# A two-layer trunk on one core: row normalisations and combined blocks at the ends of stages

## The chip, the cores and the metric

The kernel runs on one core of a Trainium2 chip. The engines of the core are TensorE (PE, matmuls), VectorE (DVE), ScalarE (ACT), GpSimd (POOL) and SyncE (SP, which issues most DMAs). Each engine works through its own queue strictly in order, and waits on semaphores for results of the others. The metric is the device time of one execution in microseconds (us), and lower is better.

## The reference

The input is one sequence of 1024 tokens, 1024 wide, in fp32, and a conditioning vector. Two layers follow each other. Each has a mixer (layer 0 a gated delta net, layer 1 a retention) and a feed-forward network, with adaptive gains; after each of the two a row normalisation is done. Cut to what the change touches:

```
DN_ALPHA = (2.0 * DEPTH) ** 0.25

def _standardize(x, eps):
    mu = jnp.mean(x, axis=-1, keepdims=True)
    xc = x - mu
    return xc * lax.rsqrt(jnp.mean(xc * xc, axis=-1, keepdims=True) + eps)

# a sublayer: residual, gained output, row normalisation
x = standardize(DN_ALPHA * x + gain * sublayer(modulated(x)))
# the feed-forward network
g, u = split(h @ ffn_up);  y = (silu(causal_dwconv(g)) * u) @ ffn_down
# after the last sublayer
out = standardize(...) * g + b
```

## The kernel before

Operands of matmuls are split into a high and a low part (`split`, L89 makes the high one by ACT, L90 the low one by DVE, or by POOL where asked), and each product is three matmuls, high by low, low by high and high by high (L110 to L112, L315 to L317, L616). Rows are tiled by 128: 8 row tiles, in two halves of four. Columns are cut in two halves of 512. PSUM tiles have the names `acc`, `sc` (accumulators) and `mm` (two banks, for transposes and short products). A scheduler has laid down the order of every engine's queue by its own estimate of when things are ready; on the chip the order is fixed.

The stages that matter, with their place in the profiled execution:

- **Delta net out projection** (`proj_ln`, L301 to L355, about 660 to 761 us). It runs for half 0 and half 1, in each for two column halves `nh`; four accumulators `accs[t]`, one for each row tile. When an accumulator is done, L345 multiplies it by the gain into `t`, and `add_row` (L283, DVE) makes ALPHA times the residual row plus `t` and, in the same instruction, the row's sum. `row_stats` (L286 to L292): DVE turns the sums into a negative mean, ACT squares both halves with an accumulated sum (L289), DVE brings that to a variance, POOL raises it to the power of minus one half (L292). `normalize` then runs on ACT (L297, 128x1024, bias from L296) or on DVE (L299). The residual rows come by DMA (`load_row`, L273) into buffers of the name `lane`. While half 1 is projected, `hooks` for half 0 are put between its groups of matmuls: transposes of the finished rows (L259, PE, into `mm`), scale and shift (L261, ACT), split into `hT` (L89, L90).
- **Start of a feed-forward network** (`strassen`, about 761 to 837 us in layer 0, 2305 to 2377 us in layer 1). The up projection is done with products of blocks, after Winograd. For the first two items both left halves are computed plainly from `hT`, while `build_T` (L373 to L418) transposes the rows of the second half (L387), scales them (L389, ACT: blocks `12` and `22`) and makes four combined blocks T1 to T4 of each `k` (L409 to L415). A sum of high and low part of a block that exists only split is made on PE by two matmuls with a unit matrix (`joined`, L395). All four combined blocks of `k` are made before those of `k + 1`. From the third item on each goes through `wino`: seven products with the blocks, of which the first two need `11` and `21`, the third T1, the fourth T2, the sixth T3, the seventh T4. Each needs a combined weight block, which DVE makes (`psub`, L1184, in an `mm` bank) and splits (L90, `wb`). Beside that, DVE works off the short convolution of the gate (L1527), the join of its halves (L1513) and adaptive gains of the next stage (`ada`, L214 and L216). The first sum in `wino` is taken when both the product in `sc` is done (L1513) and a copy by ACT.
- **End** (second part of `proj_gen`, about 2957 to 2990 us). The seventh product of the last down projection gives four accumulators one after the other, for row tiles 0 to 3 of the second half and the low column half. For each, `f4` adds it to a partial result (L1397), multiplies by the gain (L1398), `add_row` adds the residual, `norm` does `row_stats`, and the two column halves go apart: the low one by two DVE operations (L1355, L1356), the high one by ACT (L1354) and two POOL operations with gain and bias rows (L1358, L1359). Two DMAs per row tile bring them out (L1357, L1360).

Of the kernel before, what the change touches and what calls it, by code (L numbers as in the profile page):

```python
# [33 lines left out]
def trunk_kernel(ctx: ExitStack, tc, A):  # L34
# [250 lines left out]
    def row_stats(st, xt):  # L285
# [6 lines left out]
        pool.tensor_tensor(st[:, 3:4], st[:, 4:5], mhalf[:, 0:1], ALU.pow)  # L292

    def normalize(xt, st, on_act):
        if on_act:
            dve.tensor_tensor(st[:, 2:3], st[:, 2:3], st[:, 3:4], ALU.mult)  # L296
            act.activation(xt, xt, AF.Identity, bias=st[:, 2:3], scale=st[:, 3:4])  # L297
        else:
            dve.tensor_scalar(xt, xt, st[:, 2:3], st[:, 3:4], ALU.add, ALU.mult)  # L299

    def proj_ln(half, nk, get_hl, wsrc, xsrc, G, key=None, final=None, hooks=(), per=2, tag="lane", done=None):  # L301
# [5 lines left out]
        else:  # L307
            hooks = [h for p in zip(loads, hooks[:4]) for h in p] + hooks[4:] if hooks else loads
        stats = [flat(tl("st", [P, 2, 6])) for _ in range(4)]

# [8 lines left out]
        for nh in range(2):  # L319
# [21 lines left out]
            for t in range(4):  # L341
                for n, (hl, w, kk) in enumerate(tail):
                    mmt(accs[t], t, hl, w, kk, False, n == 3)
                tmp = tl("t2", [P, HALF])
                dve.tensor_mul(tmp, accs[t], G[nh])  # L345
# [26 lines left out]

    def build_T(B, xts, scale, shift, tags):  # L373
        tags = dict(zip(("T1", "T2", "T3", "T4", "22"), tags))
# [24 lines left out]
        for k, tg in enumerate((("qkv", "qkv"), ("qkv", "qkv"), ("t2", "t2"), ("t2", "ada"))):  # L399
            b12, b22 = load(k, tg[0]), load(4 + k, tg[1])  # L400
            put("12", k, b12, pool if BAL["b3"] & 1 << k else dve)
            put("22", k, b22, pool if BAL["b2"] & 1 << k else dve)
            raw.append((b12, b22))

        def rest():
            for k in range(4):
                t1, b22 = raw[k]
                x11 = joined(B["11"][k])
# [722 lines left out]

    def strassen(hT0, xts, scale, shift, items, tags=("hTb", "hTb", "qkv", "qkv", "aux"), direct=False, beside=None):
        B = {"11": hT0[:4], "21": hT0[4:]}
# [18 lines left out]
        for n in range(2):  # L1152
# [7 lines left out]
            for t, x in zip(ahead[n], X):  # L1160
                act.activation(t, x, AF.Copy)
        rest = build_T(B, xts, scale, shift, tags)

# [55 lines left out]

        bg_tag[0] = "lane"  # L1220
        for n in range(2):
# [25 lines left out]
    def proj_gen(nj, ablk, wsrc, slots, xsrc, G, final, ln_next, tag, ltags, dst, key, mm=pe.matmul, gate=None, gain=None):  # L1247
# [87 lines left out]
        def xload(half, t):  # L1335
# [32 lines left out]
        def gained(half, t, nh, c):  # L1368
            later.append(lambda: dve.tensor_tensor(c, c, G[nh], ALU.mult))
            later.append(lambda: finish(half, t, nh, c))  # L1370

        def f1(t, acc):
# [22 lines left out]

        def f4(t, acc):
            dve.tensor_tensor(p1[t], acc, p1[t], ALU.add)  # L1397
            dve.tensor_tensor(p1[t], p1[t], G[0], ALU.mult)  # L1398
            finish(1, t, 0, p1[t])
            norm(1, t)  # L1400
# [77 lines left out]
    def layer_tail(i, mix, wout, xsrc, x_mid, x_out, ln_next, final):  # L1478
        sc2, sh2 = fold(i, 1, 2 * i)
        if i == 0:  # L1480
            hT0 = []
            get = out_hl(mix)
            G1 = rows[0, 2]
            xts = proj_ln(0, GH, get, wout, xsrc, G1, ("x", i))
            hooks = ln_hooks(0, xts, "hTa", lambda: (sc2, sh2), hT0, x_mid, ("mid", i), BAL["gh"])
            xts = proj_ln(1, GH, get, wout, xsrc, G1, ("x", i), hooks=hooks)
            hooks = ln_hooks(1, xts, "hTa", lambda: (sc2, sh2), [], x_mid, ("mid", i))
            for h in hooks[KT:]:
                h()
        else:  # L1490
            mix.append((sc2, sh2))
            hT0, xts = proj_st(mix[0])
# [6 lines left out]
        ad = dr.tile([NF // 2, 7, P, HALF], F32, tag=f"ad{i}", name=f"ad{i}")  # L1499
        up = A["ffn_up"][i]  # L1500

        def pair_items(fp):
            g, o = [], []

            def gate_start():
                g.extend(tl("lane", [P, D], name="g") for _ in range(2))

# [426 lines left out]
```

## Time and profile before

| what | value |
| --- | --- |
| median of 3 runs | 2995.94 us (2995.53 to 2998.75) |
| the profiled execution | 2992.3 us |
| its span, first to last instruction | 2990.3 us |
| PE busy, share of the span | 95% |
| DVE busy | 73% |
| ACT busy | 45% |
| POOL busy | 20% |
| mean granted TensorE clock | 0.980 |

Rows of groups and of the timeline read: start, duration, engine, line, operation, output from input, shape, count, and in brackets how long the engine stood idle just before and what released it. Rows of waits read: engine, output and line, what it waited for, then us in total, times, and the longest. `L12` is line 12 of the kernel; the lines of the changed kernel are some 5 to 52 higher.

### The profile page before, as it was taken

What the parts mean: (1) busy time and instruction counts of PE and PEld (TensorE: products, weight loads), DVE (VectorE), ACT (ScalarE), POOL (GpSimd) and SP (SyncE); (2) the same over time, 40 slices, a digit from 0 to 9 for tenths busy, and PEclk for the clock granted to TensorE, in tenths of its full rate; (3) what the DMA queues carried; (4) which work ended last, traced back from release to release, by engine and by line L of the source; (5) the groups of instructions that cost most, each with busy time, mean ns of one, the idle gap of its engine ahead of it and who ended that gap; (6) DMA issues with size and microseconds to landing.
All of it is one profiled execution on the core that took longest, in us unless ns stands there. A gap on an engine that the chain in (4) does not pass through costs nothing.

```text
span 2990.3 us, 38893 instructions
## 1 busy us (share of the span) xinstructions
PE 2827.8 (95%) x13638; PEld 2308.4 (77%) x13638; DVE 2191.9 (73%) x3877; ACT 1347.4 (45%) x2513; POOL 604.6 (20%) x629
## 2 busy tenths in 40 slices
PE   8889998999999999999999989989999899999996
PEld 7768877887778888877787777767778688888785
DVE  5785687545588888997677665656687787778888
ACT  4655555434544444536443333212345544445444
POOL 0411221133011111520002330232201011112603
PEclk9999999999999999999999999999999999999998
DMA  7222221344344444864424453556573333335652
GB/s 273 86 77 72 96 89 64 117 159 137 110 141 162 155 151 147 311 204 135 154 79 145 157 210 119 170 169 183 169 248 125 127 134 106 106 106 200 242 179 106
DMA packets 235379, 442.35 MB, mean 148 GB/s; under 512 B 22192, under 2 KB 75696, under 8 KB 235184
## 3 DMA queue, kind: packets, MB, share of 16 engines
q1 hardware_dynamic: 205024, 387.96, 38.9%
q10 hardware_dynamic: 25152, 34.61, 3.2%
q0 software_dynamic: 5008, 17.30, 1.5%
q8 instruction: 107, 1.75, 0.2%
q14 instruction: 88, 0.72, 0.1%
HBM read 331.26 MB, written 108.53 MB: 147 GB/s over the span
## 4 chain that ended last, share of the span: by engine, by line
PE 68%; DVE 13%; issue 8%; DMA 6%; ACT 4%; POOL 2%; SPq 0%; POOLq 0%; ACTq 0%; DVEq 0%
PE acc L616 15%; PE acc L1412 11%; PE acc L1138 8%; PE acc L110 5%; PE acc L111 4%; PE acc L112 4%; PE sc L616 4%; PE sc L1138 3%; PE sc L1412 3%; PE mm L616 2%; PE sc L111 2%; PE sc L110 2%; PE sc L112 2%; DMA mvw<-in_ada_w 1%; DVE qkv L435 1%
## 5 line engine op out<-in xcount | busy, mean ns | idle before, releaser
L1412 PE MATMUL acc<-bb,ab 128*128 128x512 f32 x1800 | 427.7, 392 | 3.7 <-DVE bb L90 1.5
L1412 PEld LDWEIGHTS acc<-bb,ab 128*128 128x128 f32 x1800 | 337.3, 188 | 78.2 <-DVE bb L90 3.9
L616 PE MATMUL acc<-hT,wh 128*128 128x512 f32 x960 | 301.2, 395 | 0.0
L1548 POOL TENSOR_TENSOR o<-o 128x512 f32<-128x512 f32 x88 | 118.3, 1354 | 719.5 <-DVE o L1541 684.7
L1138 PE MATMUL acc<-T,wb 128*128 128x512 f32 x840 | 209.4, 400 | 12.6 <-DVE wb L90 12.6
L616 PEld LDWEIGHTS acc<-hT,wh 128*128 128x128 f32 x960 | 183.4, 191 | 33.8
L616 PE MATMUL acc<-hT,wl 128*128 128x512 f32 x480 | 203.5, 424 | 0.2 <-ACT sg L1064 0.2
L89 ACT ACTIVATE ab<-ar 128x512 fp32r<-128x512 f32 x210 | 129.4, 624 | 158.7 <-PE acc L1412 85.6
L1138 PEld LDWEIGHTS acc<-T,wb 128*128 128x128 f32 x840 | 161.2, 193 | 50.6 <-DVE wb L90 16.9
L90 DVE TENSOR_TENSOR ab<-ar,ab 128x512 fp32r<-128x512 f32 x210 | 172.9, 830 | 30.1 <-ACT ab L89 29.7
L90 DVE TENSOR_TENSOR wb<-wr,wb 128x512 fp32r<-128x512 f32 x162 | 114.2, 710 | 86.8 <-ACT wb L89 86.5
L90 DVE TENSOR_TENSOR wl<-wr,wh 128x1024 fp32r<-128x1024 f32 x85 | 104.2, 1225 | 97.3 <-ACT wh L89 97.3
L89 ACT ACTIVATE wh<-wr 128x1024 fp32r<-128x1024 f32 x101 | 106.8, 1058 | 129.9 <-PE acc L616 61.5
L90 DVE TENSOR_TENSOR wb<-mm,wb 128x512 fp32r<-128x512 f32 x216 | 145.1, 685 | 21.1 <-ACT wb L89 19.1
L1197 ACT ACTIVATE pc<-acc 128x512 f32<-128x512 f32 x143 | 84.6, 592 | 160.9 <-PE acc L1138 108.2
L89 ACT ACTIVATE wb<-mm 128x512 fp32r<-128x512 f32 x216 | 122.4, 593 | 76.5 <-DVE mm L1184 76.2
L89 ACT ACTIVATE wb<-wr 128x512 fp32r<-128x512 f32 x162 | 98.9, 626 | 98.8 <-DMA wr<-in_ffn_up 49.5
L616 PE MATMUL acc<-wh,hT 128*128 128x512 f32 x384 | 137.1, 420 | 2.5 <-DVE vv L90 1.6
L1527 DVE SCALAR_TENSOR_TENSOR o<-g,vc,o 128x512 f32<-128x512 f32 (+2 forms) x176 | 135.3, 787 | 0.9 <-ACT o L1522 0.2
L435 DVE SCALAR_TENSOR_TENSOR qkv<-raw,vc,qkv 128x512 f32<-128x512 f32 x144 | 114.8, 801 | 26.8 <-ACT qkv L433 25.5
L216 DVE SCALAR_TENSOR_TENSOR ada<-mvw,e,ada 128x512 f32<-128x512 f32 x140 | 107.1, 765 | 27.2 <-DMA mvw<-in_ada_w 27.1
L110 PE MATMUL acc<-T,wb 128*128 128x512 f32 x292 | 116.7, 400 | 9.9 <-DVE wb L90 9.4
(620 smaller groups left out, 7079.8 us busy)
## 6 DMA issues: line engine op xcount, KB each, us to landing
wr<-in_ffn_up SPq DMA_DIRECT2D x96, 512.0 KB, 4.4
mvw<-in_ada_w SPq DMA_DIRECT2D x80, 512.0 KB, 4.4
ad<-o SPq DMA_DIRECT2D x154, 256.0 KB, 2.3
ar<-ad SPq DMA_DIRECT2D x154, 256.0 KB, 4.0
Br<-in_ffn_down SPq DMA_DIRECT2D x66, 256.0 KB, 3.8
wr<-in_ret_wv SPq DMA_DIRECT2D x32, 512.0 KB, 3.9
ar<-od SPq DMA_DIRECT2D x56, 256.0 KB, 5.2
xs<-xt ACTq DMA_DIRECT2D x24, 512.0 KB, 3.1
```

What stands on the lines that cost most here:

```text
L89: act.activation(dst_h, src, AF.Copy)
L90: eng.tensor_tensor(dst_l, src, dst_h, ALU.subtract)
L110: mm(acc, wl[:, k], hl[0], start=first, stop=False)
L111: mm(acc, wh[:, k], hl[1], start=False, stop=False)
L112: mm(acc, wh[:, k], hl[0], start=False, stop=last)
L216: dve.scalar_tensor_tensor(a, wr[:, kk], e[:, k:k + 1], a, ALU.mult, ALU.add)
L435: dve.scalar_tensor_tensor(oh, raw[:, 3 - j:515 - j], w[:, 3 - j:4 - j], oh, ALU.mult, ALU.add)
L616: pq(pe.matmul(out, lhsT, rhs, start=start, stop=stop, **kw), cost)
L1138: return pe.matmul(*a, skip_group_check=True, **kw)
L1412: mm_ = (lambda *a, p=p, onto=onto, **kw: (mm if p < 2 else pe.matmul)(*a, skip_group_check=onto, **kw))
L1527: dve.scalar_tensor_tensor(tv, gv[:, c0 - j:c1 - j], w[:, 2 - j:3 - j], tv, ALU.mult, ALU.add)
L1548: pool.tensor_tensor(o[d], o[x], o[y], op)
```

## The change

Four things are changed. What is computed stays the same, apart from the order of sums.

1. In the out projection of layer 0 (`proj_ln`), a row's sum and squares are no longer made by L283, L289 and ACT. DVE adds the residual without a sum (L352 of the changed kernel), takes `bn_stats` of each column half (L353), joins them with `bn_aggr`, adds epsilon; POOL makes the power; and DVE normalises the 128x1024 row (L357), where ACT did (L297).
2. At the end, row tiles 2 and 3 of the second half use DVE alone but for POOL's power: `bn_stats`, and the gain and bias for both column halves in two operations each (L1373, L1375). Their partial result is multiplied by the gain and added to the residual ahead of the last product (`before_last`), so that after it stand L1444 (accumulator times gain), L1445 (add), L1368 (`bn_stats`).
3. The rows of half 1 in `proj_ln` lie in buffers of the name `aux` instead of `lane`, with their loads spread among the first hooks; in layer 0 the block `22` goes to `lane`, and the gate's tiles and the background tiles to `aux`.
4. `build_T` makes the combined blocks by the order of use in both feed-forward networks: T1 for all four `k`, then T2, T3, T4. T3 joins block `11` a second time, so that 24 unit-matrix matmuls stand in the start of each network instead of 16. The retention keeps the old order.

```
+    def row_bn(st, xt, mv):
+        dve.bn_aggr(mv[:, 0:2], st)
+        dve.tensor_scalar(mv[:, 2:3], mv[:, 1:2], LN_EPS, None, ALU.add)
+        pool.tensor_tensor(mv[:, 3:4], mv[:, 2:3], mhalf[:, 0:1], ALU.pow)
...
-                add_row(stats[t], nh, xv, tmp)
+                dve.scalar_tensor_tensor(xv, xv, ALPHA, tmp, ALU.mult, ALU.add)
+                dve.bn_stats(stats[t][:, nh], xv)
                 if nh == 1:
-                    row_stats(stats[t], xts[t])
-                    normalize(xts[t], stats[t], BAL["gn"] & 1 << half)
+                    mv = tl("s8", [P, 4], name="mv")
+                    row_bn(stats[t], xts[t], mv)
+                    dve.tensor_scalar(xts[t], xts[t], mv[:, 0:1], mv[:, 3:4], ALU.subtract, ALU.mult)
...
+            for k, (t1, b22) in enumerate(raw):
+                dve.tensor_sub(t1, t1, joined(B["11"][k]))
+                put("T1", k, t1)
+            for k, (t1, b22) in enumerate(raw):
                 dve.tensor_sub(b22, b22, t1)
-                put("T3", k, b22, pool if BAL["b3"] & 1 << k else dve)
-                dve.tensor_add(b22, b22, x11)
-                put("T2", k, b22, pool if BAL["bT"] & 1 << k else dve)
-                dve.tensor_sub(t1, t1, x11)
-                put("T1", k, t1, pool if BAL["b1"] & 1 << k else dve)
+                put("T2", k, b22)
+            for k, (t1, b22) in enumerate(raw):
+                dve.tensor_sub(t1, b22, joined(B["11"][k]))
+                put("T3", k, t1)
+            for k, (t1, b22) in enumerate(raw):
                 dve.tensor_sub(b22, joined(B["21"][k]), b22)
-                put("T4", k, b22, pool if BAL["b4"] & 1 << k else dve)
+                put("T4", k, b22)
...
+        def last_rows(t):
+            xt, st = xts[1][t], stats[1][t]
+            mv = tl("s8", [P, 4], name="mv")
+            dve.bn_stats(st[:, 0:6], xt[:, hs(0)])
+            row_bn(st.rearrange("p (a b) -> p a b", a=2), xt, mv)
+            (gB, bB), out = final
+            r0 = HALF + t * P
+            for h2 in range(2):
+                dve.scalar_tensor_tensor(xt[:, hs(h2)], xt[:, hs(h2)], mv[:, 0:1], gB[h2], ALU.subtract, ALU.mult)
+            for h2 in range(2):
+                dve.scalar_tensor_tensor(xt[:, hs(h2)], xt[:, hs(h2)], mv[:, 3:4], bB[h2], ALU.mult, ALU.add)
+                sp.dma_start(out[r0:r0 + P, hs(h2)], xt[:, hs(h2)])
+
+        def late(half, t):
+            return final and half and t > 1
+
+        def before_last(t):
+            lo, hi = xts[1][t][:, hs(0)], xts[1][t][:, hs(1)]
+            dve.bn_stats(stats[1][t][:, 6:12], hi)
+            dve.tensor_tensor(p1[t], p1[t], G[0], ALU.mult)
+            dve.scalar_tensor_tensor(lo, lo, ALPHA, p1[t], ALU.mult, ALU.add)
...
         def f4(t, acc):
+            if late(1, t):
+                lo = xts[1][t][:, hs(0)]
+                dve.tensor_tensor(p1[t], acc, G[0], ALU.mult)
+                dve.tensor_tensor(lo, lo, p1[t], ALU.add)
+                last_rows(t)
+                return
             dve.tensor_tensor(p1[t], acc, p1[t], ALU.add)
...
-            xts = proj_ln(1, GH, get, wout, xsrc, G1, ("x", i), hooks=hooks)
+            xts = proj_ln(1, GH, get, wout, xsrc, G1, ("x", i), hooks=hooks, tag="aux")
...
+        spare = ("aux", "lane")[i]
...
-        strassen(hT0, xts, sc2, sh2, [it for fp in range(NF // 2) for it in pair_items(fp)])
+        strassen(hT0, xts, sc2, sh2, [it for fp in range(NF // 2) for it in pair_items(fp)], ("hTb", "hTb", "qkv", "qkv", ("lane", "aux")[i]), spare=spare)
```

How the order of the queues changes is shown at three places.

**VectorE in the out projection**, where half 1's first column half ends. `hT` rows split transposed rows of half 0; L345 (L350 after the change) frees an accumulator. Before:

```order
L90 TENSOR_TENSOR hT<-t_6605,hT 128x512
L90 TENSOR_TENSOR hT<-t_6615,hT 128x512
L90 TENSOR_TENSOR hT<-t_6637,hT 128x512
L345 TENSOR_TENSOR t_6676<-acc,g_6025 128x512
L345 TENSOR_TENSOR t_6691<-acc,g_6025 128x512
L90 TENSOR_TENSOR hT<-t_6647,hT 128x512
L283 SCALAR_TENSOR_TENSOR xt,st<-xt,t_6676 128x512
```

and with the change:

```order
L357 TENSOR_SCALAR xt<-xt,mv 128x1024 x3
L90 TENSOR_TENSOR hT<-t_6503,hT 128x512
L90 TENSOR_TENSOR hT<-t_6551,hT 128x512
L350 TENSOR_TENSOR t_6616<-acc,g_6025 128x512
L352 SCALAR_TENSOR_TENSOR xt<-xt,t_6616 128x512
L353 BN_STATS st<-xt 128x6
L90 TENSOR_TENSOR hT<-t_6575,hT 128x512
L350 TENSOR_TENSOR t_6632<-acc,g_6025 128x512
L350 TENSOR_TENSOR t_6648<-acc,g_6025 128x512
L90 TENSOR_TENSOR hT<-t_6599,hT 128x512
```

Seven splits of `hT` stood ahead of the first L345, and two stand ahead of it now; the normalisation of three rows of half 0 (L357) has come in ahead of them.

**The start of the feed-forward network of layer 1**, TensorE first. `sc` is the product of blocks `21` that runs when the plain products are through, `mm` what a join leaves, and `acc<-T1` the first product with a combined block. Before, from the last join on (ten more rows of the product in `sc` follow):

```order
L395 MATMUL mm_20234<-hT_19537,ident_r_727 128x512 x2
L112 MATMUL acc_20348<-hT_19464,wb_20345 128x512
L110 MATMUL acc_20348<-hT_19474,wb_20345 128x512
L111 MATMUL acc_20348<-hT_19474,wb_20345 128x512
L112 MATMUL acc_20348<-hT_19474,wb_20345 128x512
L111 MATMUL sc_20368<-hT_19507,wb_20365 128x512
```

and with the change:

```order
L402 MATMUL mm_20218<-hT_19507,ident_r_727 128x512 x2
L110 MATMUL sc_20360<-hT_19507,wb_20357 128x512
L402 MATMUL mm_20226<-hT_19517,ident_r_727 128x512 x2
L111 MATMUL sc_20360<-hT_19507,wb_20357 128x512
L112 MATMUL sc_20360<-hT_19507,wb_20357 128x512
L110 MATMUL sc_20360<-hT_19517,wb_20357 128x512
L111 MATMUL sc_20360<-hT_19517,wb_20357 128x512
L112 MATMUL sc_20360<-hT_19517,wb_20357 128x512
L110 MATMUL acc_20379<-T1_20130,wb_20376 128x512
```

Behind the last join stood 15 matmuls up to the end of the product in `sc`; now there are five.

VectorE at the same place, up to the split of the weight block that the first product with T1 needs (`wb`, last row). Before:

```order
L415 TENSOR_TENSOR bt_20070<-mm_20234,bt_20070 128x512
L1184 TENSOR_TENSOR mm_20382<-mm_20363,wr_20341 128x512
L90 TENSOR_TENSOR T4_20239<-bt_20070,T4_20238 128x512
L1527 SCALAR_TENSOR_TENSOR o_20242<-g_20078,vc_153,o_20242 128x511
L1513 TENSOR_TENSOR g_20339<-sc_20368,pc_20361 128x512
L1527 SCALAR_TENSOR_TENSOR o_20247<-g_20078,vc_153,o_20247 128x512
L1527 SCALAR_TENSOR_TENSOR o_20242<-g_20078,vc_153,o_20242 128x510
L1527 SCALAR_TENSOR_TENSOR o_20252<-g_20079,vc_153,o_20252 128x511
L1527 SCALAR_TENSOR_TENSOR o_20257<-g_20079,vc_153,o_20257 128x512
L1527 SCALAR_TENSOR_TENSOR o_20247<-g_20078,vc_153,o_20247 128x512
L90 TENSOR_TENSOR wb_20384<-mm_20363,wb_20384 128x512
```

and with the change (ahead of these rows stand the two L436, of which the second takes `mm_20226`, one L1205 and a split of T4):

```order
L1565 TENSOR_TENSOR g_20331<-sc_20360,pc_20353 128x512
L1205 TENSOR_TENSOR mm_20374<-mm_20355,wr_20333 128x512
L90 TENSOR_TENSOR T4_20231<-bt_20050,T4_20230 128x512
L1579 SCALAR_TENSOR_TENSOR o_20234<-g_20058,vc_153,o_20234 128x511
L1579 SCALAR_TENSOR_TENSOR o_20239<-g_20058,vc_153,o_20239 128x512
L1579 SCALAR_TENSOR_TENSOR o_20244<-g_20059,vc_153,o_20244 128x511
L214 TENSOR_SCALAR ada_20431<-mvw_20432,e_162 128x512
L1579 SCALAR_TENSOR_TENSOR o_20249<-g_20059,vc_153,o_20249 128x512
L1579 SCALAR_TENSOR_TENSOR o_20234<-g_20058,vc_153,o_20234 128x510
L1579 SCALAR_TENSOR_TENSOR o_20475<-g_20331,vc_153,o_20475 128x511
L1579 SCALAR_TENSOR_TENSOR o_20239<-g_20058,vc_153,o_20239 128x512
L90 TENSOR_TENSOR wb_20376<-mm_20355,wb_20376 128x512
```

Between the row that reads `sc` (L1513, now L1565) and `wb` stood five rows, and now there are ten. In layer 0 both engines' rows stand in the same order.

**VectorE at the end of the program**, from the read of the last accumulator on. Before (the row that reads it is L1397):

```order
L1397 TENSOR_TENSOR pa<-acc,pa 128x512
L1355 SCALAR_TENSOR_TENSOR xt<-xt,st,rowb 128x512
L1398 TENSOR_TENSOR pa<-pa,rowb 128x512
L290 TENSOR_TENSOR st<-st 128x1
L283 SCALAR_TENSOR_TENSOR xt,st<-xt,pa 128x512
L291 TENSOR_SCALAR st<-st 128x1
L286 TENSOR_TENSOR st<-st 128x1
L287 TENSOR_SCALAR st<-st 128x1
L1355 SCALAR_TENSOR_TENSOR xt<-xt,st,rowb 128x512
L1353 TENSOR_TENSOR st<-st 128x1
```

and with the change, to the program's last row (the row that reads it is L1444):

```order
L1444 TENSOR_TENSOR pa<-acc,rowb 128x512
L296 TENSOR_SCALAR mv<-mv 128x1
L1373 SCALAR_TENSOR_TENSOR xt<-xt,mv,rowb 128x512 x2
L1445 TENSOR_TENSOR xt<-xt,pa 128x512
L1375 SCALAR_TENSOR_TENSOR xt<-xt,mv,rowb 128x512 x2
L1368 BN_STATS st<-xt 128x6
L295 BN_AGGR mv<-st 128x2
L296 TENSOR_SCALAR mv<-mv 128x1
L1373 SCALAR_TENSOR_TENSOR xt<-xt,mv,rowb 128x512 x2
L1375 SCALAR_TENSOR_TENSOR xt<-xt,mv,rowb 128x512 x2
```

Eleven operations of 128x512 elements lead VectorE from the last accumulator to the program's last row: seven for tile 3, and four (the first L1373 and L1375 pairs) that still belong to tile 2. Before, ACT and POOL did the high half of each of these rows.

More of the change, by code (lines that the diff above doesn't have):

```diff
@@ L308, in proj_ln @@
             hooks = [h for p in zip(loads, hooks[:4]) for h in p] + hooks[4:] if hooks else loads
-        stats = [flat(tl("st", [P, 2, 6])) for _ in range(4)]
+        stats = [tl("st", [P, 2, 6]) for _ in range(4)]
         def mmt(acc, t, hl, w, kk, first, last):
@@ L400, in build_T @@
             b12, b22 = load(k, tg[0]), load(4 + k, tg[1])
-            put("12", k, b12, pool if BAL["b3"] & 1 << k else dve)
-            put("22", k, b22, pool if BAL["b2"] & 1 << k else dve)
+            put("12", k, b12)
+            put("22", k, b22)
             raw.append((b12, b22))
         def rest():
-            for k in range(4):
-                t1, b22 = raw[k]
-                x11 = joined(B["11"][k])
-                dve.tensor_sub(b22, b22, t1)
-                put("T3", k, b22, pool if BAL["b3"] & 1 << k else dve)
-                dve.tensor_add(b22, b22, x11)
-                put("T2", k, b22, pool if BAL["bT"] & 1 << k else dve)
-                dve.tensor_sub(t1, t1, x11)
-                put("T1", k, t1, pool if BAL["b1"] & 1 << k else dve)
+            if direct:
+                for k in range(4):
+                    t1, b22 = raw[k]
+                    x11 = joined(B["11"][k])
+                    dve.tensor_sub(b22, b22, t1)
+                    put("T3", k, b22)
+                    dve.tensor_add(b22, b22, x11)
+                    put("T2", k, b22)
+                    dve.tensor_sub(t1, t1, x11)
+                    put("T1", k, t1)
+                    dve.tensor_sub(b22, joined(B["21"][k]), b22)
+                    put("T4", k, b22)
+                return
+            for k, (t1, b22) in enumerate(raw):
+                dve.tensor_sub(t1, t1, joined(B["11"][k]))
+                put("T1", k, t1)
+            for k, (t1, b22) in enumerate(raw):
+                dve.tensor_sub(b22, b22, t1)
+                put("T2", k, b22)
+            for k, (t1, b22) in enumerate(raw):
+                dve.tensor_sub(t1, b22, joined(B["11"][k]))
+                put("T3", k, t1)
+            for k, (t1, b22) in enumerate(raw):
                 dve.tensor_sub(b22, joined(B["21"][k]), b22)
-                put("T4", k, b22, pool if BAL["b4"] & 1 << k else dve)
+                put("T4", k, b22)
         return rest
@@ L1130, in c_of, with strassen @@
         return b
-    def strassen(hT0, xts, scale, shift, items, tags=("hTb", "hTb", "qkv", "qkv", "aux"), direct=False, beside=None):
+    def strassen(hT0, xts, scale, shift, items, tags=("hTb", "hTb", "qkv", "qkv", "aux"), direct=False, beside=None, spare="lane"):
         B = {"11": hT0[:4], "21": hT0[4:]}
@@ L1218, in wino @@
             bg_step()
-        bg_tag[0] = "lane"
+        bg_tag[0] = spare
         for n in range(2):
@@ L1370, in gained @@
             later.append(lambda: finish(half, t, nh, c))
+            if late(half, t):
+                later.append(lambda: before_last(t))
         def f1(t, acc):
@@ L1505, in gate_start @@
             def gate_start():
-                g.extend(tl("lane", [P, D], name="g") for _ in range(2))
+                g.extend(tl(spare, [P, D], name="g") for _ in range(2))
                 def gate(q, a, b):
```

5 lines of the change are left out of this document (3 added, 2 removed).

## The prediction

> **What bounds the kernel now.** I read the page's shares first, then TensorE's waits, then the timelines of PE and DVE at the stages that the change touches.
>
> ```profile
> PE 2827.8 (95%) x13638; PEld 2308.4 (77%) x13638; DVE 2191.9 (73%) x3877; ACT 1347.4 (45%) x2513; POOL 604.6 (20%) x629
> ```
>
> TensorE is busy for 95% of the span, so a change that leaves its matmuls alone can only take out its gaps. The waits of PE from 700 to 870 us (us in total, times, longest) cover the out projection and the start of the first feed-forward network:
>
> ```profile
> PE acc L110 <- DVE wb L90: 4.7, 1, 4.7
> PE acc L315 <- DVE t L345: 3.2, 2, 2.5
> PE mm L259 <- ACT t L261: 2.6, 3, 1.1
> PE mm L387 <- ACT bt L389: 2.1, 1, 2.1
> PE acc L1138 <- DVE wb L90: 1.9, 1, 1.9
> ```
>
> The first and last row belong to the combined blocks; the second and third are the out projection, the fourth the first transposes of the network. PE's timeline shows what the longest wait in the out projection brings with it:
>
> ```profile
> 735.73 0.80 PE L315 MATMUL acc<-wh,hl 128*128 128x512 f32 x1 [2.46 <-DVE t L345]
> 736.32 0.63 PE L316 MATMUL acc<-wl,hl 128*128 128x512 f32 x1
> 736.75 0.63 PE L317 MATMUL acc<-wh,hl 128*128 128x512 f32 x1
> ...
> 741.87 0.44 PE L317 MATMUL acc<-wh,hl 128*128 128x512 f32 x1
> 742.14 0.39 PE L315 MATMUL acc<-wh,hl 128*128 128x512 f32 x1
> 742.37 0.39 PE L316 MATMUL acc<-wl,hl 128*128 128x512 f32 x1
> ```
>
> After 2.46 us of waiting the matmuls follow each other at 0.43 us until 741.87, and then at 0.23: some 15 matmuls lose 0.2 us each, 3.0 us on top of the wait. [...]
>
> **The change part by part.**
>
> *(a) Out projection.* DVE's rows ahead of that matmul:
>
> ```profile
> 733.78 1.29 DVE L90 TENSOR_TENSOR hT<-t,hT 128x512 fp32r<-128x512 f32 x2 [1.08 <-ACT hT L89]
> 734.99 1.28 DVE L345 TENSOR_TENSOR t<-acc,g 128x512 f32<-128x512 f32 x2
> ```
>
> L345, which frees the accumulator, stood behind seven splits of `hT`, each waiting for ACT. With the change two are ahead of it, so it can run some five splits (5 x 0.64 = 3.2 us) sooner, which is more than the wait of 2.46. If so, wait and slow matmuls go: 2.46 + 3.0 = 5.5. Of the 2.6 us of L259's waits on ACT I take a fifth, 0.5, since the transposes now stand in smaller groups. What DVE gets for it, per row tile two `bn_stats` and a normalisation, costs by their nearest rows:
>
> ```profile
> L1761 DVE BATCH_NORM_STATS2 rst<-sc x32: 685/699/700, 1836.2 to 2161.4; 128x6 f32<-128x512 f32 x32
> L299 DVE TENSOR_SCALAR xt<-xt,st x12: 806/812/816, 1447.0 to 2318.2; 128x1024 f32<-128x1024 f32 x12
> 727.00:761.00 34.00, 28.84 (x122) 22.74 (x121) 13.01 (x25) 11.47 (x16) 7.15 (x3) 0.90 0.40 137
> ```
>
> That is 2 x 0.70 + 0.81 = 2.2 us a tile, 18 us for eight tiles over two halves; in the window row (DVE's busy time is the third, 13.01 of 34 us) they fit in idle time. Three normalisations (2.4 us) are now ahead of L350, however: if they come late, since each waits for POOL's power, the wait stays. So -6, from -9 (3.2 + 2.6 + 3.0, all of it) to -2 (only the lesser waits go).
>
> DVE and POOL do hold each other up:
>
> ```profile
> 702.44 2.39 POOL L90 TENSOR_TENSOR wl<-wr,wh 128x1024 fp32r<-128x1024 f32 x1 [3.04 <-ACT wh L89]
> 702.47 2.92 DVE L283 SCALAR_TENSOR_TENSOR xt<-xt,t 128x512 f32<-128x512 f32 x1
> ```
>
> An L283 that starts with POOL's split ends with it, 2.92 us where other operations of its size take 0.69 (L1513, below). L352, in its place, has the same two operands in SBUF, and keeps that price; `bn_stats` and L357 have one. [...]
>
> *(b) Buffers at the first network's start.*
>
> ```profile
> 785.83 1.79 PE L387 MATMUL mm<-cst,xt 128*128 128x128 f32 x8 [2.08 <-ACT bt L389]
> ```
>
> ```profile
> PE mm L387 <- ACT bt L389: 0.7, 1, 0.7
> ```
>
> The first row is from PE's timeline, the last from PE's waits from 2300 to 2400 us, the same place in layer 1. In layer 0 ACT's first two block builds stood behind both last copies of the plain products (L1161); with the rows in other buffers they come ahead of the last copy, as they already did in layer 1, where PE waits 0.7. The wait of 2.08 and some half-clock matmuls behind it go: -2.5, from -3.5 to 0.
>
> *(c) Combined blocks by use.* Here the change costs, twice. PE and DVE at layer 1's start, before:
>
> ```profile
> 2360.22 0.62 PE L395 MATMUL mm<-hT,ident_r 128*128 128x512 f32 x2
> 2360.68 0.40 PE L112 MATMUL acc<-hT,wb 128*128 128x512 f32 x1
> ...
> 2363.89 0.39 PE L112 MATMUL sc<-hT,wb 128*128 128x512 f32 x1
> 2368.97 0.80 PE L110 MATMUL acc<-T,wb 128*128 128x512 f32 x1 [4.69 <-DVE wb L90]
> 2376.27 1.10 PE L1138 MATMUL acc<-T,wb 128*128 128x512 f32 x3 [2.17 <-DVE wb L90]
> ```
>
> ```profile
> 2364.32 0.69 DVE L1513 TENSOR_TENSOR g<-sc,pc 128x512 f32<-128x512 f32 x1
> 2364.93 3.39 DVE L1527 SCALAR_TENSOR_TENSOR o<-g,vc,o 128x512 f32<-128x512 f32 x5
> 2368.23 0.68 DVE L90 TENSOR_TENSOR wb<-mm,wb 128x512 fp32r<-128x512 f32 x1
> 2368.83 0.48 DVE L214 TENSOR_SCALAR ada<-mvw,e 128x512 f32<-128x512 f32 x1
> ```
>
> PE's product ends at 2364.28, DVE reads it at 2364.32 and needs five L1527 (0.66 each) before `wb`. PE waits for `wb` alone; T1 is there. What changes, for one network:
>
> 1. Eight more joins on PE, which is dense here: two take 0.46 (2360.22 to 2360.68), eight 1.8 us.
> 2. The last join stands five matmuls before the product's end instead of 15, so it is done only some 1.1 us before it. Behind it DVE has the second L436 (to 0.5 before the end), L1205 and a split of T4 (0.6 each, to 0.7 after), then L1565, L1205 and a split (1.8, to 2.5), seven L1579 at 0.66 (4.6), L214 (0.4) and `wb` (0.7): 8.2 us after the product's end, where it was 4.7. So 3.5 more.
> 3. Nine instead of eleven rows are then left between this `wb` and the next: the gap of 2.17 shrinks by about 1.0.
> 4. Joins now follow each other in two `mm` banks with DVE's subtraction between them; by DVE's 0.6 a row I add 0.3.
>
> Together 1.8 + 3.5 - 1.0 + 0.3 = 4.6 for each network, and 9.2 for both. Bounds for one: 1, if the stretch's own stalls and DVE's lead take up most of it; 7, if the twelve matmuls after the second gap run at half clock too (12 x 0.2 = 2.4 more). T1 being ready sooner wins nothing, as T1 was never waited for.
>
> *(d) End.* PE, DVE, POOL and the last DMA, before:
>
> ```profile
> 2956.49 13.22 PE L616 MATMUL acc<-bb,ab 128*128 128x512 f32 x57 [0.16 <-DVE ab L90]
> 2971.00 1.21 DVE L1353 TENSOR_TENSOR st<-st 128x1 f32<-128x1 f32 x1
> 2972.80 0.68 DVE L1397 TENSOR_TENSOR pa<-acc,pa 128x512 f32<-128x512 f32 x1
> 2974.92 1.75 DVE L1398 TENSOR_TENSOR pa<-pa,rowb 128x512 f32<-128x512 f32 x1
> 2970.94 1.26 POOL L1359 TENSOR_TENSOR xt<-xt,rowb 128x512 f32<-128x512 f32 x1
> 2974.53 1.59 POOL L1359 TENSOR_TENSOR xt<-xt,rowb 128x512 f32<-128x512 f32 x1
> 2985.79 1.26 POOL L1359 TENSOR_TENSOR xt<-xt,rowb 128x512 f32<-128x512 f32 x1
> ```
>
> PE ends at 2969.71, DVE reads the last accumulator only at 2972.80, and POOL ends the rows at 2987.05, 17.3 us after PE; the remaining 3.25 us to the span's end are the last DMA, and stay. DVE is late because POOL holds it: a 128x1 operation takes 1.21 us beside POOL's L1359, and L1398 1.75 instead of 0.69. With the change eleven operations of 512 elements lead from the last accumulator to the last row, at 0.66 from start to start 7.3, and 0.3 for the small ones; POOL's power lies beside L1373. If DVE is there when PE ends, rows end at 2977.4, 9.7 earlier. If it is as late as before (2972.80) and the four POOL operations left for tiles 0 and 1 stall it three times by 1.0, they end at 2983.4, 3.6 earlier. I take the middle, -6.5.
>
> *Sum* against the profiled execution: 2992.3 - 6 - 2.5 + 9.2 - 6.5 = 2986.5. The runs' median lies 3.6 above that execution, so 2990.1.
>
> **The rivals.**
>
> - *R1, by use costs nothing.* DVE's rows ahead of `wb` fall into idle time, the joins into PE's old stalls. For it: DVE had waits in this stretch, and a row moved ahead of `wb` is one less behind it. Against it: DVE read `sc` 0.04 us after PE was done, so there is no lead to use up. Without (c): 2990.1 - 9.2 = 2980.9.
> - *R2, POOL's splits hold VectorE.* The moved work makes DVE's queue in the out projection the bound: L352 beside POOL's split takes 2.2 us more, and L350 of the next tile is behind it. With four such meetings, (a) is -6 + 8.8 = +2.8; at the end the stalls stay (-3.6). It decides when the meetings lie on the last two row tiles of a column half, where PE waits for the accumulator. 2992.3 + 2.8 - 2.5 + 9.2 - 3.6 = 2998.2, with the distance to the median 3002: slower.
> - *R3, the loads or L357 come late*, so that the out projection's long wait and slow clock stay: (a) -1 instead of -6: 2995, no change.
>
> **How the numbers follow.** Forecast 0.45, R1 0.28, R2 0.12, R3 0.15. A difference under 0.2% (6 us) can't be told from none. The forecast's own range is 2984 to 2996 and its middle lies at that border: half of it is faster, half is the same. Faster: 0.22 + nearly all of R1, 0.26 = 0.48. Same: 0.22 + 0.14 + 0.03 = 0.39, with what is left of R1 and R3. Slower: R2 and a tail of the forecast, 0.13. The range reaches from R1 to near R2: 2979 to 3000.
>
> **What would show it.** (a): no wait of over 1 us of L315 on DVE between 727 and 745 us, matmuls at 0.23 there. (b): PE's first wait at L394 under 1 us. (c): the gap before the first product with T1 about 8 us at both networks, 24 joins in each, the next gap near 1. (d): the last DVE row 10 to 12 us after PE's end. The forecast falls if the gap before `wb` stays at 4.7 (R1), if an L352 of over 2 us stands ahead of a waiting L315 (R2), or if half-clock matmuls follow the out projection's first column half (R3).

## The result and the profile after

| | the change | the kernel before | ratio, 95% interval | difference |
| --- | --- | --- | --- | --- |
| first timing | 2976.25 us (2971.39 to 2984.12, 6 runs) | 2995.74 us (2987.61 to 2998.75, 6 runs) | 0.994 (0.9923 to 0.9957) | -18 us (-23 to -13) |
| second timing (e9 below) | 2978.99 us (2973.36 to 2990.69, 7 runs) | 2992.01 us (2988.15 to 3001.08, 12 runs) | 0.9954 (0.9937 to 0.9971) | -14 us (-19 to -9) |

The change is faster by some 14 to 18 us. Forecast were 6. The ratios differ a little from the quotient of the medians.

The profiled execution of the changed kernel took 2971.39 us (span 2969.6) and is the fastest of its six; that of before took 2992.3. To see where the 20.7 us between the spans lie, the two traces are compared by the times at which the same matmuls start. Stage bounds are the first and the last L315 (out projection), the first transpose of `build_T` (L387), the last matmul before the wait for `wb`, the first product with T1, the first product with `22` in `wino` (network's start), and the end of TensorE's last matmul.

| stage | before, us | after less before | forecast |
| --- | --- | --- | --- |
| out projection | 103.69 | -9.25 | -6 |
| first network's start, whole | 68.78 | -0.49 | -2.5 + 4.6 |
| ... transposes to the wait for `wb` | 52.16 | -1.63 | |
| ... the wait for `wb` | 5.08 | +3.57 | +3.5 |
| ... from there to the product with `22` | 11.54 | -2.43 | -1.0 |
| second network's start, whole | 66.30 | +1.98 | +4.6 |
| after TensorE's last matmul | 20.63 | -5.70 | -6.5 |
| sum of these | | -13.46 | -5.8 |
| everything else | | -7.3 | 0 |

TensorE's longest waits of the changed kernel from 690 to 870 us, in the columns of the rows shown before (us in total, times, longest):

```profile
PE acc L110 <- DVE wb L90: 8.3, 1, 8.3
PE mm L259 <- DVE xt L357: 1.2, 1, 1.2
PE mm L402 <- DVE bt L427: 1.0, 1, 1.0
PE acc L321 <- POOL wl L90: 0.8, 1, 0.8
PE acc L1159 <- DVE wb L90: 0.8, 1, 0.8
PE mm L394 <- ACT bt L396: 0.7, 1, 0.7
```

No wait for the accumulators (3.2 us before) is left, and the transposes L259 no longer wait for L261 (2.6 before); a wait of 1.2 us for the new normalisation and one of 0.8 us are what the out projection still has. The wait of 2.1 us at the first transposes is gone too. The wait for `wb` has grown from 4.7 to 8.3 us.

VectorE at the end of half 1's first column half:

```profile
720.01 0.69 DVE L90 TENSOR_TENSOR hT<-t,hT 128x512 fp32r<-128x512 f32 x1 [4.85 <-ACT hT L89]
721.48 2.47 DVE L90 TENSOR_TENSOR hT<-t,hT 128x512 fp32r<-128x512 f32 x1 [0.77 <-ACT hT L89]
724.05 0.69 DVE L350 TENSOR_TENSOR t<-acc,g 128x512 f32<-128x512 f32 x1
```

Two splits, and then the accumulator is read, although the second split, beside one of POOL from 721.01 to 723.41, took 2.47 us (the first took 0.69). The granted clock stays at 1.00 from 725 to 745 us, where it was 0.67 from 736 to 745 before, and 0.50 while the slow matmuls of before ran (735.73 to 741.87).

TensorE at the first network's wait for `wb`, first of the changed kernel, then of before:

```profile
819.91 0.80 PE L110 MATMUL acc<-T,wb 128*128 128x512 f32 x1 [8.26 <-DVE wb L90]
820.50 0.63 PE L111 MATMUL acc<-T,wb 128*128 128x512 f32 x1
...
824.77 0.63 PE L112 MATMUL acc<-T,wb 128*128 128x512 f32 x1
826.15 3.03 PE L1159 MATMUL acc<-T,wb 128*128 128x512 f32 x12 [0.76 <-DVE wb L90]
```

```profile
833.84 0.52 PE L112 MATMUL acc<-T,wb 128*128 128x512 f32 x1
836.27 4.45 PE L1138 MATMUL acc<-T,wb 128*128 128x512 f32 x12 [1.92 <-DVE wb L90]
```

The first twelve products run at 0.43 us each in both, at a granted clock of 0.50 (819.9 to 825.0 and, before, 828.5 to 834.0). Behind them the changed kernel waits 0.76 us instead of 1.92, and its next twelve take 3.03 us instead of 4.45: before, most of those ran at the half clock too (granted 0.64 from 836.27 to 840.7; in the changed kernel 1.00 from 826.15 to 829.2).

The end, VectorE and POOL; TensorE's last matmul of the changed kernel ends at 2954.67:

```profile
2952.36 1.25 DVE L290 TENSOR_TENSOR st<-st 128x1 f32<-128x1 f32 x1
2954.94 1.21 DVE L1396 TENSOR_TENSOR st<-st 128x1 f32<-128x1 f32 x1
2956.85 0.63 DVE L1444 TENSOR_TENSOR pa<-acc,rowb 128x512 f32<-128x512 f32 x1
2957.47 2.13 DVE L1373 SCALAR_TENSOR_TENSOR xt<-xt,mv,rowb 128x512 f32<-128x512 f32 x2
2959.52 1.74 DVE L1445 TENSOR_TENSOR xt<-xt,pa 128x512 f32<-128x512 f32 x1
2964.86 1.41 DVE L1375 SCALAR_TENSOR_TENSOR xt<-xt,mv,rowb 128x512 f32<-128x512 f32 x2
```

```profile
2954.87 1.26 POOL L1402 TENSOR_TENSOR xt<-xt,rowb 128x512 f32<-128x512 f32 x1
2957.12 1.26 POOL L1401 TENSOR_TENSOR xt<-xt,rowb 128x512 f32<-128x512 f32 x1 [0.99 <-ACT xt L1397]
2959.31 1.40 POOL L1402 TENSOR_TENSOR xt<-xt,rowb 128x512 f32<-128x512 f32 x1
```

The rows end at 2966.27, 11.6 us after TensorE (17.3 before), and the last transfer takes 3.3 us as it did. VectorE reads the last accumulator 2.2 us late, and POOL's remaining operations hold it up at L290, L1396, L1373 and L1445.

### The profile page after: what moved, and what is told of

Read it like the earlier page. It is cut to its first block, busy times and chain, and to the rows that moved or that the text cites. A ratio compares the mean times of both kernels' runs of the same rounds, so it can differ in the third digit from the quotient of the medians.

```text
span 2969.6 us, 38837 instructions
## 1 busy us (share of the span) xinstructions
PE 2819.0 (95%) x13654; PEld 2302.7 (78%) x13654; DVE 2214.7 (75%) x3863; ACT 1323.3 (45%) x2463; POOL 598.5 (20%) x625
## 4 chain that ended last, share of the span: by engine, by line
PE 67%; DVE 15%; DMA 7%; issue 6%; ACT 3%; POOL 1%; SPq 0%; DVEq 0%; ACTq 0%; POOLq 0%
PE acc L637 15%; PE acc L1463 9%; PE acc L1159 8%; PE acc L110 5%; PE acc L111 5%; PE acc L112 5%; PE sc L1159 4%; PE sc L637 4%; PE sc L1463 2%; PE mm L637 2%; PE sc L110 2%; PE sc L111 2%; PE sc L112 2%; DMA mvw<-in_ada_w 1%; DVE qkv L456 1%
```

## The experiments

The theory on record was that the by-use order costs 4.6 us at each network, and that the rows and buffers and the end earn 15. Its first rival (R1) was that by use costs nothing. After the result a third reading was added: the untouched stages, which differ by 7.3 us between the two profiles, differ like that from one execution to the next. The experiments take the four parts of the change apart. "Less before" is, as above, stage by stage from the profiles; timings are against the kernel before on the same chip.

| kernel | out projection | first network's start | second network's start | after TensorE's end | timed, us (interval) |
| --- | --- | --- | --- | --- | --- |
| whole change | -9.25 | -0.49 | +1.98 | -5.70 | -18 (-23 to -13) |
| e9, whole change again | -9.28 | -0.52 | +2.00 | -5.71 | -14 (-19 to -9) |
| e1, without by use | -9.25 | -3.07 | +1.09 | -4.58 | -22 (-28 to -16) |
| e2, by use only | +0.27 | +3.92 | +4.35 | -0.40 | +6 (+2 to +10) |
| e3, rows and buffers | -9.25 | -2.96 | -1.99 | -1.10 | -15 (-20 to -10) |
| e4, end only | -1.05 | -0.09 | -0.25 | -4.60 | -6 (-11 to -1) |
| e5, rows only | -1.47 | -2.95 | -0.96 | -1.08 | -4 (-9 to 0) |
| e6, buffers only | -8.78 | -0.05 | +0.15 | -0.64 | -11 (-16 to -7) |
| e7, as e1, `wb` early | -9.25 | -3.31 | +0.06 | -4.25 | -16 (-22 to -10) |
| e8, as e7, all rows | -9.29 | -4.50 | -0.08 | -8.25 | -20 (-26 to -13) |
| e10, as e1, all rows | -9.29 | -3.09 | +0.87 | -8.63 | -19 (-24 to -14) |

**e1 to e4, the parts.** e1 takes back the by-use order:

```
         def rest():
-            if direct:
+            if True:
                 for k in range(4):
```

e2 is the kernel before with that order alone, e3 has the first and the third part of the change, e4 the second alone.

> The change without its by-use order (rows by bn statistics, other buffers and the end stay). Theory 1, as predicted: by use costs 4.6 us at each of the two network starts, so that this kernel is 9 us faster than the whole change, some 27 us below the kernel before, with the wait of TensorE for wb at 4.7 us instead of 8.3. Theory 2: the longer wait is made good behind it by shorter waits; then this kernel is within 3 us of the whole change, 15 to 21 us below before.

> The kernel before with the by-use order alone, in both networks. Theory 1: 9 us slower than before, with a wait for wb of about 8 us at each network's start. Theory 2: the same wait, but the time within 3 us of before, since later waits in the same stretch shrink by as much.

> The kernel before with the out projection's rows by bn statistics and with the other buffers. By the two profiles: out projection 9 us shorter, first network's start 2 to 3 us shorter, so 11 to 12 us below before. If a further part of the 18 us comes from the down projection and the retention because work there meets other transfers, 18 us; if what those stages differ by is variation from one execution to the next, 12.

> The kernel before with the last two row tiles by VectorE alone. By the two profiles 4.7 us below before, all of it after the last matmul; predicted were 6.5. Everything ahead of the last product is the same order as before, so the stages from the first network's down projection to the end of the retention show how far two executions of the same order differ: if by 7 us as between the two profiles, their difference is variation.

By use alone is slower, 6 us (2 to 10), and its two starts are 3.9 and 4.4 us longer; R1 falls. TensorE's waits in e2 that belong to the combined blocks, at the first network and then for `wb` at the second:

```profile
PE acc L110 <- DVE wb L90: 8.3, 1, 8.3
PE mm L400 <- DVE bt L425: 1.0, 1, 1.0
PE acc L1157 <- DVE wb L90: 0.8, 1, 0.8
```

```profile
PE acc L110 <- DVE wb L90: 6.7, 1, 6.7
PE acc L1157 <- DVE wb L90: 2.2, 1, 2.2
```

So the longer wait is real, and 8.3 us is what the walk through VectorE's rows had given (8.2). At the first network two thirds of the 3.57 us more come back: the next wait falls from 1.9 to 0.8 and the half clock ends sooner (the twelve products behind that wait took 4.45 us before and 3.03 in the whole change). At the second network 2.06 us more are waited, and 0.38 come back. Without by use (e1) the first wait is that of before, and the second somewhat longer (2.7 against 1.9); the stretch from the first to the product with `22` is as long as before (+0.09):

```profile
PE acc L110 <- DVE wb L90: 4.7, 1, 4.7
PE acc L1159 <- DVE wb L90: 2.7, 1, 2.7
```

e1 was timed at -22 against -18 and -14 of the whole change; the intervals overlap, so the timing alone does not settle that e1 is the faster one, nor which of the two theories on record holds (9 us, or within 3). Its two starts are together 3.5 us shorter than those of the whole change (-3.07 against -0.49, +1.09 against +1.98); e10 against e9 gives 3.7 in the same way. But e3, whose matmuls stand at both starts in the same order as those of e1, gives 6.4. At the second start these two differ by 3.1 us, which is therefore no effect of the order. e1 waits 1.33 us for `wl` at the start's first product, and e3 does not; and behind the second wait for `wb` the products run at full clock in e3 (first row) and mostly at half clock in e1 (second row):

```profile
2357.48 3.02 PE L1159 MATMUL acc<-T,wb 128*128 128x512 f32 x12 [1.81 <-DVE wb L90]
```

```profile
2367.66 4.61 PE L1159 MATMUL acc<-T,wb 128*128 128x512 f32 x12 [2.31 <-DVE wb L90]
```

So inside the whole change by use costs 3.5 to 6.4 us, depending on the kernel it is compared with, where e2 puts it at 8.3 alone.

e4 gains what the profile shows after TensorE's end (-4.60). Its order up to the last product is that of before.

**What is left over.** None of the stages that the change was meant to alter lies between the end of the first network's up projection and the start of the second network (1091 us). Against before this stretch was -5.7 us in the whole change and -1.0 in the same kernel's second profile (e9). In e2, e4, e5 and e6 the matmuls stand there in just the order of before, and it was -6.5, -2.2, +1.6 and -1.4. In the other kernels a few of its 4605 matmuls stand elsewhere, late in the stretch; from there on the two profiles of the whole change lose or gain under 0.5 us against before. The start of the out projection came between 1.8 us earlier and 13.7 us later (e7).

The touched stages of the whole change repeat within 0.05 us in e9, but that is no rule. The out projection of e4, in the order of before, is 1.05 us shorter; and the first starts of e7 and e8, in the same order of matmuls, differ by 1.2 us, by the clock: the twelve products behind their second wait for `wb` took 5.49 us in e7 and 4.30 in e8. The 7.3 us are therefore read as variation of the untouched stages: in e9 the span is 14.8 us below before, and 13.5 of these are in the touched stages. Over the eleven rows of the table the timed difference and the sum of the four stages are up to 6 us apart (e1), and on average less than 1; an effect of a microsecond or two elsewhere is not excluded.

**e5 and e6, which part pays the out projection.** In the order of e5 seven splits of `hT` still stand ahead of L350 (L345 before), in e6 two. That tells apart what makes the wait. Of the diff the first piece is e5, the second e6 (with the blocks and tiles that change places).

```
-                add_row(stats[t], nh, xv, tmp)
+                dve.scalar_tensor_tensor(xv, xv, ALPHA, tmp, ALU.mult, ALU.add)
+                dve.bn_stats(stats[t][:, nh], xv)
...
-            xts = proj_ln(1, GH, get, wout, xsrc, G1, ("x", i), hooks=hooks)
+            xts = proj_ln(1, GH, get, wout, xsrc, G1, ("x", i), hooks=hooks, tag="aux")
```

> The kernel before with the out projection's rows by bn statistics alone; the rows of half 1 stay in the old buffers. In its order seven splits of hT still stand ahead of the first L350. If the splits ahead of L350 make the wait of 2.46 us and the slow matmuls, both stay, and the out projection gains at most 2 us (the smaller waits at 706 and 716 us of before). If the statistics make the gain, it is the 9 us of the whole change.

> The kernel before with the other buffers alone, sums and squares of rows still by ACT. In its order two splits stand ahead of the first read of an accumulator. If these splits make the wait, the out projection is 7 to 8 us shorter and the network's start 3 to 5 us (no wait of 2.1 us at the first transposes): 10 to 13 us in all. If the statistics make the gain, only the network's start is shorter: 3 to 5 us.

Of TensorE's waits, from 700 to 800 us in e5, and from 690 to 790 us in e6:

```profile
PE acc L320 <- DVE t L350: 3.9, 2, 3.8
PE mm L259 <- ACT t L261: 2.0, 1, 2.0
PE mm L259 <- DVE xt L357: 1.1, 1, 1.1
PE mm L394 <- ACT bt L396: 0.7, 1, 0.7
```

```profile
PE mm L392 <- ACT bt L394: 2.1, 1, 2.1
PE acc L320 <- DVE t L350: 0.8, 1, 0.8
PE mm L259 <- ACT xt L302: 0.6, 1, 0.6
```

With statistics alone the wait for the accumulator stays, even longer (3.8 us), and the stage gains 1.5 us, little more than the 1.05 that e4 gained in the order of before. With buffers alone it is gone (the 0.8 us are an earlier wait, at 706 us, which before had too), and the stage gains 8.8. So the other buffers, with which the last load is issued at 708 us (e6) instead of 734 (before) and the hooks spread, pay the out projection. At the network's start it is the other way round, against what was expected of e6: the wait of 2.1 us at the first transposes is there in e6 and gone in e5. There the statistics pay: in e5 ACT starts its first two blocks at 780.48, ahead of the last copy of the plain products (785.18), and in e6 behind that copy. That the order came out so because ACT is rid of squares and normalisations is likely, but no run shows it by itself.

**e7 and e8, the wait for `wb` and the rows at the end.** e7 writes the first product with T1 ahead of the short convolution; e8 adds the last row of the diff, by which all four row tiles of the second half end on VectorE; e10 is e1 with that row.

```
             Z = prod(s1, "T1")
+            yield
...
+            if late_conv:
+                first = wino(2, items[2][2]())
+                next(first)
+                items[0][3]()
...
-            return final and half and t > 1
+            return final and half
```

> The change without its by-use order (as e1_no_by_use), and with the first combined product written ahead of the short convolution of the gate, so that two instead of five L1527 (here L1590) stand between the read of sc and the split of wb. If the rows of VectorE ahead of wb set TensorE's wait, it falls from 4.7 to about 2.7 us at both networks, and some of the half-clock matmuls behind it go too: 4 to 9 us below e1_no_by_use, some 28 us below before. If the later rows only move the wait to the next weight block, nothing is won.

> As e7_no_by_use_wb_early, and at the end all four row tiles of the second half by VectorE alone instead of two, so that POOL multiplies nothing there. If what POOL holds VectorE up by was the rest of the end's time, the stalled rows (1.2 us for a 128x1 operation, 1.7 for a 512 one) go, and the last row of VectorE ends 9 to 10 us after TensorE's last matmul instead of 11.6 to 12.7: 2 to 3 us. If VectorE's own rows set the end, four more operations for tiles 0 and 1 make it no faster.

In e7 the wait for `wb` falls to 2.7 us as expected, but of the 2.0 us at each network little is left at the stage's end (0.2 and 1.0 us against e1; 1.4 and 1.0 for e8 against e10), and the timing is not below that of e1:

```profile
828.32 0.58 PE L110 MATMUL acc<-T,wb 128*128 128x512 f32 x1 [2.71 <-DVE wb L90]
...
836.40 5.49 PE L1159 MATMUL acc<-T,wb 128*128 128x512 f32 x12 [3.46 <-DVE wb L90]
```

The rows of VectorE that were passed are now ahead of the next weight block: the second wait is 3.46 us instead of 2.7, and the twelve products behind it run at half clock (5.49 us). The two waits together are 6.2 us, where they were 7.4 in e1; the half clock behind the second takes most of the difference (the same twelve products took 4.48 us in e10, whose first start stands in the order of e1).

e8 and e10 end 4.0 us sooner than e7 and e1 after TensorE's last matmul (-8.25 against -4.25, -8.63 against -4.58), where 2 to 3 were expected. In e10 POOL has only the powers left, and no row of VectorE is stretched:

```profile
2957.41 0.68 DVE L1444 TENSOR_TENSOR pa<-acc,rowb 128x512 f32<-128x512 f32 x1
2958.13 0.69 DVE L1445 TENSOR_TENSOR xt<-xt,pa 128x512 f32<-128x512 f32 x1
2962.34 1.41 DVE L1373 SCALAR_TENSOR_TENSOR xt<-xt,mv,rowb 128x512 f32<-128x512 f32 x2
2963.66 1.41 DVE L1375 SCALAR_TENSOR_TENSOR xt<-xt,mv,rowb 128x512 f32<-128x512 f32 x2
```

L1445 is back at 0.69 us from 1.74, the L1373 pair at 1.41 from 2.13, and this although VectorE does at least four operations more: what POOL had held it up by was larger.

**e9 and e10, beside each other.**

> The whole change once more, beside the next kernel on one chip. By the sum of the stages that it touches (out projection -9.3, first network's start with both orders -0.5, second network's start +2.0, end -5.7, by the profiles against before) 13 to 14 us below before. If something in the untouched stages is gained as well, 18 us or more, as the first timing had it.

> The change without its by-use order, and with all four row tiles of the second half at the end by VectorE alone (the weight block of the first combined product stays where it was). By the stages: out projection -9.3, first network's start -3, second 0, end -8: 20 us below before, and 6 us below the whole change on the same chip. If the by-use order costs nothing, only the end's 2.5 us.

On one chip the whole change came out at 2978.99 us and e10 at 2972.28 (2970.21 to 2978.97), -14 and -19 us against before, as the stages say (-13 and -20). Their intervals overlap, and so the 5 to 7 us between them are shown by the stages, and by the timing only as likely. e1, e8 and e10 have the largest timed gains (-22, -20 and -19); the timings do not tell these three apart, and all lie clear of the kernel before.

## Why the prediction was wrong

The direction was forecast right, the size was not: 6 us were forecast and 14 to 18 came. No rival describes it; R1 came nearest in time, for a reason that did not hold. By its own steps:

- **(a) out projection: mechanism right, term mis-sized, -6 forecast, -9.25 measured.** The splits ahead of the accumulator's read were the cause (e5 against e6), and the 2.46 us and the half clock behind them went as forecast. The other waits were booked too low. TensorE waited 7.1 us in this stage (the 3.2 and 2.6 shown, and 1.3 in three smaller rows) and waits 2.0 now, so that 5.1 us went where 3.0 were booked. Of L259's 2.6 us of waits on ACT only a fifth had been booked, and all of it went: 24 of these transposes stood one behind the other, and now at most eight do (in e6 too, which has no such wait; in e5 it is 16, and the wait is 2.0 us). The last 1.1 us of the stage's gain is not put down to a row. The doubt that three normalisations ahead of L350 would keep the wait was unfounded: the last pair ended at 715.17, 4.8 us ahead of the first split. It was also left open which part moves the splits; it is the buffers.
- **(b) first network's start: -2.5 forecast, some -3 measured (e1, e3, e5), but the cause was wrong.** The step put it on the buffers. With buffers alone nothing happens up to the wait for `wb` (-0.28), with statistics alone all of it (-3.15).
- **(c) by use: 9.2 forecast; 8.3 by the stages alone, 6 (2 to 10) timed alone, and 3.5 to 6.4 inside the change.** This is the step that failed. With (b) it made the two starts 6.7 us longer, and they became 1.5 us longer; no other part was so far off. Its signs came: 8.26 us at both networks, 24 joins, and next gaps of 0.76 and 1.29. Its largest piece was right: 3.5 us more at the wait, measured 3.57 in three of four places (2.06 at the second network of e2). Too little was given back behind the wait: 1.0 forecast for the second wait, 2.4 and 2.6 measured in the whole change, because the step saw a shorter gap and not that the half clock would end with it (1.4 of the 2.4). It took the twelve products behind that gap to be at full clock, and put half clock there as its upper bound; but they were mostly at half clock in the kernel before (4.45 us against 3.03). The joins, 2.1 with their handshake, were +2.8 and +2.7 in e2, but 1.5 at each start inside the change (against e1 at the first, against e3 at the second).
- **(d) end: -6.5 forecast, -5.70 measured.** The middle between both ends was a choice and not a mechanism, and that it came near is in part luck: VectorE was 2.2 us late, and two rows were stretched by 1.8 us together after that. Alone (e4) the end gave 4.60.
- **The base.** The sum was turned into a median by the 3.6 us between the profiled execution and the median of three runs shown, 2995.94. Later medians of the kernel before were 2991.6 to 2995.7, over 6 to 23 runs. Against those the forecast's 2990 stood for 1.5 to 5.6 us. The range's lower end, 2979, lies just above the first median, 2976, and at the second.
- **R2** had POOL's splits hold VectorE on the path. Three L352 did run beside such a split and took 1.47, 1.83 and 2.42 us instead of 0.68, but TensorE waited for none of them. One meeting reached TensorE, at the first normalisation, and the price was a wait of 1.2 us and not four of 2.2:

```profile
710.10 2.38 POOL L90 TENSOR_TENSOR wl<-wr,wh 128x1024 fp32r<-128x1024 f32 x1
...
710.16 2.86 DVE L357 TENSOR_SCALAR xt<-xt,mv 128x1024 f32<-128x1024 f32 x1 [0.38 <-POOL mv L297]
...
713.08 0.44 PE L259 MATMUL mm<-cst,xt 128*128 128x128 f32 x2 [1.16 <-DVE xt L357]
```

Columns are start, duration, engine, line and operation; the last row is TensorE's. L357 has one tensor operand in SBUF. The prediction gave POOL's price to L352, which has two, and none to L357; the L357 at 710.16, beside POOL's split, paid it as well: 2.86 us, against 0.76 for the one at 707.99, and it ended at 713.02, 0.5 us after POOL's split (712.48).

So the sum was off on the same side by 3.3 us in (a) and by 5.2 in (b) and (c), the two starts together; against that stand 0.8 in (d). The profile's own values give -13.5, and with the base at the later medians of before 2978 to 2982. That the first median, 2976, lies below even that is not put down to any stage of the change.

## What to carry to other kernels

When an accumulator's release stands in a queue, count the rows ahead of it that wait for a third engine: moving the loads so that these rows spread was worth six times what cheaper statistics were in that stage (8.8 against 1.5 us, the latter hardly above the variation). A longer wait at one place of an in-order queue is not a cost by itself; follow the rows that were moved to the next wait behind it, and the clock too: of 3.57 us more at the first wait, 2.43 came back behind it. And before a difference of a few us is read from two profiles, look at a stage that has the same order in both: here one of 1091 us differed from before by -6.5 to +1.6 us, and short ones by 1 to 3 us, in one place with the same matmuls behind a wait at half clock in one execution and at full clock in the other (twelve in 4.61 us in e1 and in 3.02 in e3).

## What the runs showed of the hardware

- A wait of 2.71 us (e7) was followed by matmuls at 0.43 us, as the 2.46 us before; waits of 1.16 and 0.80 us in the out projection of the changed kernel were not (granted clock 1.00 from 655 to 749 us). At the first network, after a wait of 8.26 us no more matmuls ran at half clock than after 4.69: twelve at 0.43, and then full speed, where before most of the next twelve were slow as well.
- Two of VectorE's operations of one element per partition waited for POOL as well at the end of the changed kernel (L290 1.25 us and L1396 1.21 instead of 0.15). Both ended when POOL's operation did: L290 at 2953.61 and POOL's L1401 at 2953.60, L1396 at 2956.15 and POOL's L1402 at 2956.13. L296, of the same size, took 0.14 us at 2957.41, while POOL's next L1401 ran (2957.12 to 2958.38).
- The length of a wait alone did not decide whether the clock fell. At one place of the retention, the same product follows a wait of 3.35 us in the kernel before (first row) and one of 3.42 us in e1 (second row). The granted clock was 0.77 in the 7.5 us around the first, and 1.00 in the 8 us around the second:

```profile
1734.22 4.61 PE L1138 MATMUL acc<-T,wb 128*128 128x512 f32 x12 [3.35 <-DVE wb L90]
```

```profile
1724.75 3.02 PE L1159 MATMUL acc<-T,wb 128*128 128x512 f32 x12 [3.42 <-DVE wb L90]
```
